# Counting TensorE's change of row count in an emission planner, and moving the adds of one norm's sums of squares

## The chip, the core and the metric

The kernel runs on one core of one Trainium2 chip. Five engines work side by side, each on its own queue in strict order: TensorE (matmuls and transposes, called PE in the profile, PEld for its weight loads), VectorE (DVE), ScalarE (ACT), GpSimd (POOL) and SyncE (SP), which issues the DMAs. The metric is the time of one execution on the device in microseconds. The time of a kernel is the median of several runs.

## The reference

Two layers over 512 tokens of width 1024, one after the other. Each layer takes a token norm, one input projection, a token mixer together with a cross-attention into 256 memory tokens, an output projection with a residual, and then a dense feed-forward with a norm of its own. The mixer of the first layer is chunked retention, that of the second differential attention with six heads of two 64-wide halves.

```python
def rms_norm(x, w):
    x32 = x.astype(jnp.float32)
    y = x32 * lax.rsqrt(jnp.mean(x32 * x32, axis=-1, keepdims=True) + EPS)
    return (y * w.astype(jnp.float32)).astype(x.dtype)
...
    for layer in range(DEPTH):
        h = rms_norm(x, attn_norm_w[layer])
        u = h @ w_in[layer]
...
        sc = jnp.einsum('bihcd,bjhcd->bhcij', qblk, k).astype(jnp.float32) * scale
        p = jax.nn.softmax(sc, axis=-1)
        a = p[:, :, 0] - lam * p[:, :, 1]
...
        x = x + jnp.concatenate([o_main, o_mem], axis=-1) @ w_out[layer]
        h = rms_norm(x, ffn_norm_w[layer])
        gu = h @ w_gate_up[layer]
        x = x + (jax.nn.silu(gu[..., :FFN_DIM]) * gu[..., FFN_DIM:]) @ w_down[layer]
```

All inputs are float32. The token norm sums squares over the 1024 features of each token.

## The kernel before

Activations lie transposed: eight tiles `xT[k]` of 128 features by 512 tokens. Every float32 factor is split into a rounded high part and a remainder (`split_h` on ScalarE, `split_l` mostly on VectorE), and a product is three matmuls: high by high, high by low, low by high (`mm3`). Weights come in chunks of up to 128x1024 through three raw pages (`wr`), are split into pages `wh` and `wl` (three each), and then used. The chunk after next can be loaded only when an earlier one has been split.

The order of the instructions on every engine is made by a planner when the program is written. `Weave` keeps an estimated clock for each engine. The main stream issues TensorE's projections; after each matmul of `mm3`, `W.pump()` runs every side stream (a Python generator: a split, a norm, an attention unit) whose due time lies no more than 0.1 us ahead of TensorE's estimated clock. The due times come from the estimated ends of earlier instructions plus a hand-over (`DELAY`). `Engine.go` (the estimate of TensorE stands at L269 to L271) gives each instruction its estimated duration: for a matmul with 64 rows (contracted partitions) 0.11 + 0.00012 n us, n its columns. Nothing of the estimate runs on the chip, where semaphores alone hold instructions back; but the estimate decides which instruction stands behind which.

Matmuls on 64 rows stand only in the second layer's differential attention: `unit` (L1132) computes the scores of one of six heads and one of four blocks of 128 queries, with both halves of a head in one call of `mm3_pair`: six matmuls, alternating between the upper and the lower 64 partitions. There are 24 such calls. Behind each follow a minimum on VectorE, two exponentials on ScalarE, a combination on VectorE, and for every second block transposes and the products with the values on TensorE. A `lane` starts the next unit only when VectorE's and ScalarE's estimated clocks are at most 4 us ahead of TensorE's (`W.backlog()`).

The first token norm is that of `norms[0]`, the only `NormX` with `later` set (4.0 us). For each tile `xT[k]`, `NormX.tile` (L613) splits the scaled tile into two `xw` pages, yields for `later`, draws one of three `tab` pages, squares the tile on ScalarE, and adds the square to the running sum, the first square's page, on GpSimd (L630). The planner's `take(tab=1)` keeps at most two further squares under way. After the eighth square `token_norm` multiplies the sum by ones on TensorE (eight small float32 passes) to sum over the features. The matmuls of the input projection meanwhile read the unnormed `xw`; the norm is applied behind them. The first block of the projection, `v1`, uses four chunks of 24 matmuls each.

`token_halves` (L1343) prepares operands for the feed-forward products of both layers: for each of four pairs of tiles, five intermediate results `z[0]` to `z[4]`, each half a `wk` page wide. It counts three pages, and draws six at L1357, since the page is drawn inside the inner loop.

Of the kernel before, what the change touches and what calls it, by code (L numbers as in the profile page):

```python
# [15 lines left out]
ALU = mybir.AluOpType  # L16
AX = mybir.AxisListType

P = 128
D = 1024  # L20
T = 512
# [128 lines left out]
def free_size(ap):  # L150
    n = 1
    for d in ap.shape[1:]:
        n *= d
    return n


class Weave:
# [7 lines left out]
    def __init__(self):  # L165
        self.n, self.q = 0, []
        self.clock = {"pe": 0.0, "dve": 0.0, "act": 0.0, "pool": 0.0, "dma": 0.0}
        self.written = {}
        self.slots, self.slot, self.seen = {}, {}, {}
        self.port = {"dve": [], "pool": []}  # L170
        self.last = self.cur = self.now = 0.0

    @property
# [80 lines left out]
class Engine:  # L254
# [5 lines left out]
    def __getattr__(self, op):  # L260
        call = getattr(self.engine, op)

        def go(out, *args, **kw):
            named = [v for k, v in kw.items() if isinstance(v, bass.AP) and k != "accum_out"]
            ins = [v for v in args if isinstance(v, bass.AP)] + named
            outs = [out] + [v for k, v in kw.items() if k == "accum_out"]
            n = free_size(ins[0] if op == "tensor_reduce" else out)
            if self.name == "pe":
                us = max(0.108, n / 2400 * (1 if op == "transpose" or kw["rhs"].dtype == F32R else 4) + 0.0134)  # L269
                if ins[0].shape[0] == 64:  # L270
                    us = 0.11 + 0.00012 * n  # L271
            elif self.name == "act":
                us = 0.09 + 0.00084 * n + 0.19 * ("accum_out" in kw) + 0.05 * isinstance(kw.get("scale"), bass.AP)
            elif self.name == "pool":
                us = 0.3 + 0.165 * n if kw.get("op") == ALU.pow else 0.17 + 0.0021 * n
            elif self.name == "dma":
                us = n * P * 4 / 360e3
            else:
                us = 0.07 + 0.00104 * n + 0.06 * any(free_size(v) == 1 and n > 1 for v in ins[1:])
            if self.name == "dma":  # L280
                self.weave.clock["dma"] = max(self.weave.clock["dma"], self.weave.t, self.weave.now)
            wide = [v for v in ins if free_size(v) > 1 or n == 1]
            here = [not v.tensor.name.startswith("ps_") for v in wide]
            double = sum(here) > 1 or op == "tensor_scalar" and all(here)
            port = self.name == "pool" or self.name == "dve" and double
            self.weave.run(self.name, us, outs, ins, port)
            return call(out, *args, **kw)  # L287

        return go
# [3 lines left out]
def body(ctx: ExitStack, tc: tile.TileContext, x_d, mem_d, w_d, par_d, dec_d, ali_d, out_d):  # L293
# [5 lines left out]
    V, A, G = Engine(W, "dve", nc.vector), Engine(W, "act", nc.scalar), Engine(W, "pool", nc.gpsimd)  # L299
# [8 lines left out]
    def page(tag, shape, bufs, dt=F32):  # L308
        z = sb.tile(shape, dt, tag=tag, name=nm(tag), bufs=bufs)
        W.page(tag, bufs, region(z[:, 0:1])[0])  # L310
        return z
# [12 lines left out]
    def take(**tags):  # L324
        n = tags.get("ps", 0)
        while True:
            if any(free[tag] < n_ for tag, n_ in tags.items()):
                yield 0.3
                continue
            due = max(heapq.nsmallest(n, banks), default=0.0) + 0.2  # L330
            if not n or due <= max(W.now, W.t) + EARLY:
                break
            W.cur = due
            yield
        for tag, n in tags.items():
            free[tag] -= n

    def give(tag, n):
        free[tag] += n
        if tag == "ps":  # L340
            for _ in range(n):
                heapq.heappush(banks, W.last)

    def wk(shape, dt=F32):
        return page("wk", shape, CAP["wk"], dt)
# [7 lines left out]
    def tab(shape):  # L353
        return page("tab", shape, 3)
# [35 lines left out]
    def col(c):  # L390
        return par[:, c:c + 1]
# [48 lines left out]
    def split(*parts):  # L440


        for dH, _, *src in parts:
            split_h(dH, *src)
        yield
        for p in parts:
            split_l(*p)
# [90 lines left out]
    def xw_page():  # L538
        return page("xw", [P, T], 2 * KT, F32R)
# [4 lines left out]
    def token_norm(srcs, ntok, out, bc=False, sq_sum=None, after=lambda: None):  # L544


        n = ntok // P
        if sq_sum is None:
            yield from take(tab=2)
            sq_sum = tab([P, T])  # L550
            A.activation(sq_sum, srcs[0], AF.Square)
            for src in srcs[1:]:
                sq = tab([P, T])
                A.activation(sq, src, AF.Square)
                yield
                G.tensor_tensor(sq_sum, sq_sum, sq, op=ALU.add)
            G.tensor_tensor(sq_sum[:, :ntok], sq_sum[:, :ntok], sq_sum[:, ntok:], op=ALU.add)
            give("tab", 1)
            after()
        W.cur = W.ready(sq_sum)  # L560
        yield
        yield from take(ps=1)
        pr = bank()
        for t in range(n):
            TE.matmul(pr[:, t:t + 1], lhsT=sq_sum[:, t * P:(t + 1) * P], rhs=ones[:, 0:1], start=True, stop=True)
        give("tab", 1)
        yield
        m, e, r = [page("r", [P, TT], 10)[:, :n] for _ in range(3)]
        V.tensor_scalar(m, pr[:, :n], 1.0 / D, EPS, op0=ALU.mult, op1=ALU.add)
        V.tensor_scalar(e, m, EPS, None, op0=ALU.mult)  # L570
        give("ps", 1)
        yield
        power(r, m, n)
        out.em, out.r = e, r
        if bc:
            yield from free_norm(out, out)
# [26 lines left out]
    class NormX:  # L603
# [9 lines left out]
        def tile(self, k):  # L613
            W.cur = W.ready(xT[k])
            yield
            h_, l_ = xw_page(), xw_page()
            yield from split((h_, l_, xT[k], col(self.c + k)))
            self.xw[k] = h_, l_
            while k > 0 and self.sums == 0:
                yield 0.3  # L620
            if self.later:
                yield self.later
            yield from take(tab=1)
            sq = tab([P, T])
            A.activation(sq, xT[k], AF.Square)
            if k == 0:
                self.sq_sum = sq
            else:
                yield
                G.tensor_tensor(self.sq_sum, self.sq_sum, sq, op=ALU.add)  # L630
                give("tab", 1)
            self.sums += 1
            if self.sums == KT:
                W.add(token_norm(None, T, self.nrm, self.bc, self.sq_sum), 0.0)
# [708 lines left out]
    def token_halves(layer, norm, tb):  # L1343


        room = []
        for tag, n, bufs in (("v", 3, 8), ("qc", KH, 2)):
            for z in [page(tag, [P, n, HT], bufs, F32R) for _ in range(bufs)]:
                room += [z[:, i, :] for i in range(n)]
        a, b = slice(0, HT), slice(HT, T)  # L1350
        def sums(j):
            while KH + j not in norm.xw:
                yield 0.5
            x1, x2 = xT[j], xT[KH + j]
            w1, w2 = col(norm.c + j), col(norm.c + KH + j)
            yield from take(wk=3)
            z = [wk([P, T])[:, s] for _ in range(3) for s in (a, b)]  # L1357
            A.activation(z[1], x1[:, b], AF.Copy, scale=w1)
            V.tensor_tensor(z[0], x1[:, a], x1[:, b], op=ALU.subtract)
            yield  # L1360

            V.scalar_tensor_tensor(z[2], x2[:, b], w2, z[1], op0=ALU.mult, op1=ALU.subtract)
            V.scalar_tensor_tensor(z[3], x1[:, a], w1, z[2], op0=ALU.mult, op1=ALU.add)
            V.scalar_tensor_tensor(z[4], x2[:, a], w2, z[3], op0=ALU.mult, op1=ALU.subtract)
            parts = [(room.pop(), room.pop(), *src) for src in ((z[0], w1), (z[2],), (z[3], -1.0), (z[4], -1.0))]
            yield
            for part in parts:
                yield from split(part)
            give("wk", 3)
            tb[j] = [part[:2] for part in parts]  # L1370

        for j in range(KH):
            W.add(sums(j), 0.0)
            yield 3.0
# [358 lines left out]
```

## Time and profile before

| | us |
|---|---|
| median of 3 runs | 1141.38 |
| lowest and highest run | 1139.38 and 1141.46 |
| profiled execution, its own time | 1143.51 |
| profiled execution, span from first to last instruction | 1141.7 |

| engine | busy us | share of the span |
|---|---|---|
| PE | 1130.7 | 99% |
| DVE | 892.6 | 78% |
| ACT | 626.8 | 55% |
| POOL | 157.8 | 14% |

The span lies 1.8 us under the profiled execution's own time, and that time 2.1 us above the median. A row of the timeline gives the start, the duration, the engine, the operation with what it writes and reads, how many like it stand together, and in brackets the idle time before it and what ended that. Durations of matmuls are modelled and overlap: the distance from one start to the next tells more. A row of the stretches gives each engine's busy time with its instructions, the clock granted to TensorE (1.00 is 2.4 GHz, 0.50 is 1.2 GHz) and the DMA's share.

### The profile page before, as it was taken

To read this page: it belongs to the slowest core of one execution; us is meant where nothing else is said; L and a number is where in the kernel's file an instruction comes from. 1 tells how busy PE (TensorE), PEld (TensorE's weight loads), DVE (VectorE), ACT (ScalarE), POOL (GpSimd) and SP (SyncE) were. 2 spreads that over 40 slices of the span, in tenths; PEclk is the share of its full clock that TensorE was granted. 3 is DMA by queue.
4 is the path that set the end of the run, shared out by engine and by line. 5 is a ranking of instruction groups with operands and counts; after the bars stand their busy time and mean duration, and the time that the engine had idled before them with its cause. 6 is when DMAs were issued, how large, how long until landed. Compare 5 with 4: busy or idle time off the path is not lost.

```text
span 1141.7 us, 18447 instructions
## 1 busy us (share of the span) xinstructions
PE 1130.7 (99%) x6917; PEld 999.2 (88%) x6917; DVE 892.6 (78%) x1717; ACT 626.8 (55%) x1291; POOL 157.8 (14%) x105
## 2 busy tenths in 40 slices
PE   9999999999999999999999999999999999999998
PEld 7788888889999999998888877888899999999987
DVE  5669895799997878887657577967989987788862
ACT  6557773545564445555466575745556554455540
POOL 4120010400000000000362653343000000000000
PEclk9999999999999999999999999999999999999999
DMA  6341222332342333334231311122332333223332
GB/s 212 126 143 61 74 74 75 111 93 92 118 136 84 103 110 102 97 112 159 68 116 58 111 61 51 57 74 93 94 108 89 125 105 123 86 93 102 96 111 76
DMA packets 46600, 113.54 MB, mean 99 GB/s; under 512 B 5296, under 2 KB 17968, under 8 KB 46512
## 3 DMA queue, kind: packets, MB, share of 16 engines
q1 hardware_dynamic: 46368, 112.35, 30.5%
q8 instruction: 54, 0.88, 0.3%
q14 instruction: 34, 0.28, 0.1%
q10 hardware_dynamic: 144, 0.03, 0.0%
HBM read 110.26 MB, written 2.10 MB: 98 GB/s over the span
## 4 chain that ended last, share of the span: by engine, by line
PE 91%; DVE 3%; ACT 3%; POOL 1%; issue 1%; DMA 1%; SPq 0%; DVEq 0%; ACTq 0%
PE ps L287 91%; DVE wk L287 1%; POOL tab L287 1%; ACT wk L287 1%; DVE sm L287 1%; DMA wr<-w_t 1%; ACT wh L287 0%; DVE qk L287 0%; ACT qk L287 0%; ACT mkY L287 0%; DVE mkL L287 0%; SPq L287 0%; ACT L287 0%; ACT qc L287 0%; ACT xw L287 0%
## 5 line engine op out<-in xcount | busy, mean ns | idle before, releaser
L287 PE MATMUL ps<-xw,wh 128*128 128x256 f32 (+1 forms) x1032 | 211.6, 326 | 0.0
L287 ACT ACTIVATE wk<-ps 128x256 f32<-128x256 f32 (+3 forms) x214 | 90.8, 427 | 168.2 <-PE ps L287 167.2
L287 PE MATMUL ps<-xw,wl 128*128 128x256 f32 (+1 forms) x948 | 179.0, 306 | 0.0
L287 PEld LDWEIGHTS ps<-xw,wh 128*128 128x128 f32 x1032 | 154.4, 190 | 15.5
L287 PE MATMUL ps<-wh,xw 128*128 128x512 f32 (+1 forms) x512 | 151.1, 375 | 1.0 <-DVE qk L287 1.0
L287 PEld LDWEIGHTS ps<-xw,wl 128*128 128x128 f32 x948 | 131.2, 190 | 7.4
L287 PE MATMUL ps<-qk,wl 128*128 128x512 f32 (+1 forms) x528 | 135.6, 386 | 0.0
L287 ACT ACTIVATE wh<-wr 128x512 fp32r<-128x512 f32 (+1 forms) x144 | 118.6, 827 | 27.2 <-PE ps L287 20.9
L287 DVE TENSOR_TENSOR wl<-wk,wl 128x512 fp32r<-128x512 f32 (+3 forms) x150 | 94.4, 630 | 29.0 <-ACT wl L287 28.2
L287 PEld LDWEIGHTS ps<-qk,wl 128*128 128x128 f32 x528 | 96.1, 188 | 18.3
L287 ACT ACTIVATE wl<-wk 128x512 fp32r<-128x512 f32 (+3 forms) x150 | 85.6, 571 | 40.1 <-DVE wk L287 25.7
L287 PEld LDWEIGHTS ps<-wh,xw 128*128 128x128 f32 x512 | 92.8, 191 | 16.5 <-DVE qk L287 1.5
L287 POOL TENSOR_TENSOR tab<-tab,tab 128x512 f32<-128x512 f32 x31 | 47.2, 1524 | 431.9 <-DVE v L287 306.7
L287 PE MATMUL ps<-v,wh 128*128 128x256 f32 x792 | 106.1, 279 | 0.0
L287 PE MATMUL ps<-qk,wh 128*128 128x512 f32 (+1 forms) x393 | 104.4, 387 | 0.5 <-DVE qk L287 0.5
L287 DVE TENSOR_TENSOR wh<-wk,wh 128x512 fp32r<-128x512 f32 (+3 forms) x130 | 79.2, 609 | 26.7 <-ACT wh L287 26.7
L287 PEld LDWEIGHTS ps<-v,wh 128*128 128x128 f32 x792 | 98.3, 189 | 0.0
L287 PE MATMUL ps<-wl,xw 128*128 128x512 f32 (+1 forms) x256 | 96.0, 375 | 0.9 <-DVE wl L287 0.9
L287 ACT ACTIVATE wh<-wk 128x512 fp32r<-128x512 f32 (+3 forms) x130 | 72.6, 559 | 42.5 <-DVE wk L287 34.6
L287 DVE TENSOR_TENSOR xT<-ps,xT 128x512 f32<-128x512 f32 (+1 forms) x81 | 55.1, 680 | 50.9 <-PE ps L287 50.6
L287 PEld LDWEIGHTS ps<-qk,wh 128*128 128x128 f32 x393 | 71.9, 188 | 15.6 <-DVE qk L287 1.1
L287 PE MATMUL ps<-v,wl 128*128 128x256 f32 x576 | 77.4, 279 | 0.0
(169 smaller groups left out, 1969.7 us busy)
## 6 DMA issues: line engine op xcount, KB each, us to landing
wr<-w_t SPq DMA_DIRECT2D x148, 512.0 KB, 3.5
wk<-w_t SPq DMA_DIRECT2D x48, 192.0 KB, 3.8
wk<-w_t SPq DMA_DIRECT2D x32, 256.0 KB, 3.9
wk<-w_t SPq DMA_DIRECT2D x32, 128.0 KB, 3.4
wr<-w_t SPq DMA_DIRECT2D x8, 256.0 KB, 5.2
xT<-x_t SPq DMA_DIRECT2D x8, 256.0 KB, 5.5
zo<-mem_t SPq DMA_DIRECT2D x8, 256.0 KB, 6.0
out_t<-xT SPq DMA_DIRECT2D x7, 256.0 KB, 2.0
```

Source lines behind the costliest of these rows:

```text
L287: return call(out, *args, **kw)
```

## The change

Three edits. The planner's estimate of a TensorE instruction grows by 0.19 us whenever its row count differs from that of the instruction ahead of it. The running sum of squares of the first token norm is added by VectorE in place of GpSimd; the other three such norms keep GpSimd. `token_halves` draws three pages and uses both halves of each.

```diff
@@ Weave.__init__
+        self.rows = 128
@@ Engine.go
                 if ins[0].shape[0] == 64:
                     us = 0.11 + 0.00012 * n
+
+                us += 0.19 * (ins[0].shape[0] != self.weave.rows)
+                self.weave.rows = ins[0].shape[0]
@@ NormX.tile
-                G.tensor_tensor(self.sq_sum, self.sq_sum, sq, op=ALU.add)
+                (V if self.later else G).tensor_tensor(self.sq_sum, self.sq_sum, sq, op=ALU.add)
                 give("tab", 1)
@@ token_halves
-            z = [wk([P, T])[:, s] for _ in range(3) for s in (a, b)]
+            z = [w[:, s] for w in [wk([P, T]) for _ in range(3)] for s in (a, b)]
```

## Rows read from the trace of the kernel before

**Rows 1.** The page's first part: busy time and share of the span.

```profile
PE 1130.7 (99%) x6917; PEld 999.2 (88%) x6917; DVE 892.6 (78%) x1717; ACT 626.8 (55%) x1291; POOL 157.8 (14%) x105
```

**Rows 2.** Stretches: length; busy PE, PEld, DVE, ACT, POOL; clock; DMA share; GB/s.

```profile
23.00:27.00 4.00, 2.80 (x13) 1.90 (x13) 3.56 (x3) 2.30 (x3) 2.52 (x2) 0.88 0.36 92
27.00:33.00 6.00, 6.00 (x15) 4.74 (x16) 2.98 (x8) 1.54 (x6) 2.04 (x2) 0.51 0.73 248
80.00:135.00 55.00, 53.45 (x280) 44.49 (x279) 50.78 (x101) 40.12 (x89) 4.11 (x4) 1.00 0.26 87
200.00:230.00 30.00, 30.00 (x138) 24.93 (x137) 22.50 (x33) 16.68 (x31) 12.50 (x8) 1.00 0.38 114
255.00:520.00 265.00, 265.00 (x1917) 250.31 (x1916) 228.07 (x420) 140.30 (x291) 0.00 (x0) 1.00 0.33 105
640.00:765.00 125.00, 123.24 (x769) 98.84 (x769) 99.10 (x293) 82.36 (x223) 57.13 (x32) 1.00 0.23 72
```

**Rows 3.** Timeline of TensorE, 20 to 34 us.

```profile
22.53 0.62 PE L287 MATMUL ps<-wh,xw 128*128 128x512 f32 x2
...
23.21 0.74 PE L287 MATMUL ps<-wh,xw 128*128 128x512 f32 x2
24.52 0.50 PE L287 MATMUL ps<-wl,xw 128*128 128x512 f32 x1 [0.57 <-DVE wl L287]
25.66 1.52 PE L287 MATMUL ps<-ones,tab 128*128 128x1 f32 x8 [0.63 <-POOL tab L287]
27.03 1.20 PE L287 MATMUL ps<-wh,xw 128*128 128x512 f32 x2
...
33.04 0.39 PE L287 MATMUL ps<-wl,xw 128*128 128x512 f32 x1
```

**Rows 4.** Timeline of ScalarE, 8 to 45 us.

```profile
21.42 0.61 ACT L287 ACTIVATE wh<-wr 128x512 fp32r<-128x512 f32 x1
22.25 0.63 ACT L287 ACTIVATE tab<-xT 128x512 f32<-128x512 f32 x1 [0.22 <-POOL tab L287]
22.79 2.51 ACT L287 ACTIVATE wh<-wr 128x512 fp32r<-128x512 f32 x3
```

**Rows 5.** Timeline of VectorE, 8 to 45 us.

```profile
15.96 0.99 DVE L287 SCALAR_TENSOR_TENSOR xw<-xT,par,xw 128x512 fp32r<-128x512 f32 x1 [0.72 <-ACT xw L287]
22.07 0.70 DVE L287 TENSOR_TENSOR wl<-wr,wh 128x512 fp32r<-128x512 f32 x1 [5.11 <-ACT wh L287]
23.43 4.38 DVE L287 TENSOR_TENSOR wl<-wr,wh 128x512 fp32r<-128x512 f32 x3 [0.67 <-ACT wh L287]
```

**Rows 6.** Timeline of GpSimd, 8 to 45 us.

```profile
14.88 10.72 POOL L287 TENSOR_TENSOR tab<-tab,tab 128x512 f32<-128x512 f32 x7 [13.57 <-ACT tab L287]
```

**Rows 7.** VectorE's groups by shape, 22 to 28 us, then 190 to 230.

```profile
L287 DVE TENSOR_TENSOR wl<-wr,wh 128x1024 fp32r<-128x1024 f32 x2 | 3.4, 1750 | 0.0
...
L287 DVE TENSOR_TENSOR wl<-wr,wh 128x1024 fp32r<-128x1024 f32 x7 | 8.5, 1219 | 0.4 <-ACT wh L287 0.4
```

**Rows 8.** Tile tab, VectorE: count, shortest, median and longest ns.

```profile
L287 DVE TENSOR_TENSOR wk<-wk,tab x38: 691/692/694, 265.5 to 1099.7; 128x512 f32<-128x512 f32 x38
```

**Rows 9.** The chain of work that ended last: start, length, what.

```profile
14.80 0.07 issue
```

**Rows 10.** Timeline of TensorE, 223 to 227 us.

```profile
224.60 0.95 PE L287 MATMUL ps<-ones,tab 128*128 128x1 f32 x8
225.41 0.49 PE L287 MATMUL ps<-xw,wl 128*128 128x512 f32 x1
```

**Rows 11.** Timeline of TensorE, 655 to 662 us.

```profile
656.91 0.39 PE L287 MATMUL ps<-wl,xw 128*128 128x512 f32 x1
657.23 0.79 PE L287 MATMUL ps<-qk,qk 64*128 64x384 f32 x6
657.95 0.73 PE L287 MATMUL ps<-wh,xw 128*128 128x512 f32 x2
658.52 0.27 PE L287 MATMUL ps<-ident,wk 128*128 128x128 f32 x1
```

## The prediction

> **What bounds the kernel now.** I read the page first: TensorE is busy 99% of the span, so only three things can move the time: TensorE's own work, stretches where it waits, and its clock [rows 1]. The change removes no matmul. I then cut the span into stretches and looked for TensorE idle time and a granted clock below 1.00 [rows 2]. The long feed-forward stretches (255 to 520 us stands for both layers) hold no idle time at all; VectorE is busy for 228 of those 265 us, but beside TensorE. Idle time stands in three places. From 80 to 135 us there are 1.55 us of it, spread over several waits. From 640 to 765 us, the second layer's differential attention, there are 1.76 us. And between 23 and 33 us something larger happens: 1.2 us of idle time in four microseconds, and then six microseconds at a granted clock of 0.51, that is almost all of it on the lower level, 1.2 GHz. It is the only stretch of the table far below 1.00.
>
> The timelines of that stretch tell why. TensorE runs three 512-column matmuls in 0.68 us, 0.227 us each, until 23.2 us; then it waits for a weight remainder from VectorE, then at 25.66 us for the sums of squares from GpSimd, and from 27.03 us on each matmul takes twice as long, up to 32.5 us or so [rows 3]. On ScalarE the squares of the token norm (tile tab) and the splits of the weights (tile wh) share one queue. Only three tab pages exist, one of them the running sum, so a square waits until GpSimd has added an earlier one; the split of the fourth weight chunk stands behind such squares and starts only at 21.42 us, its second half at 22.79 us [rows 4]. VectorE sits idle for 5.11 us before that, waiting for this split, and then needs 4.38 us for three remainders [rows 5]. GpSimd's seven adds take 10.72 us from 14.88 us on, 1.53 us each [rows 6]. While GpSimd adds, VectorE's own work on two SBUF operands is slower as well: a 128x1024 remainder took 1.75 us in this stretch and 1.22 us in another [rows 7]. So one chain, seven slow adds, sets the late weights, the late norm and, behind both, the fallen clock.
>
> **The adds move from GpSimd to VectorE** (the condition on `later` holds for the first token norm alone). Gone: seven adds of 1.53 us. New: seven VectorE adds of two SBUF tiles of 128x512; the nearest rows are 38 instructions of this shape at 0.69 us [rows 8]. From the first add at 14.88 us: seven adds at 0.69 us are 4.8 us, seven hand-overs of 0.07 us (the gap that the chain of waits shows between the end of a square and GpSimd's add [rows 9]; I take it for VectorE too) 0.5 us, and one input split of 0.99 us that VectorE has to do in between [rows 5]: the last sum is there at about 21.2 us, against 25.6 us. VectorE has the room, in its 5.11 us of waiting. Behind the adds, which now wait for ScalarE's squares, stand on VectorE's queue that input split and the remainders of the fourth chunk. TensorE needs that chunk at about 22.5 us, its second half at 23.2 us; the squares ahead of the split then wait for adds of 0.69 us, so the split should come near 20 us and the remainder near 21.5 us, a margin of about one microsecond. GpSimd has nothing else until the power of the norm, and no DMA is moved past another.
>
> What TensorE gets back: from 23.21 to 27.03 us stand three 512-column matmuls and eight small ones of the norm. At the upper clock the same eight took 0.81 us in the next norm [rows 10], so the stretch needs 0.68 + 0.81 = 1.49 us of 3.82 us: 2.3 us back. From 27.03 to 33.04 us stand 14 matmuls (five rows of two and four rows of one on the timeline, of which the first and the end are shown); 14 x 0.227 = 3.2 us of 6.0 us: 2.8 us back if the clock stays up. Together **5.2 us**. The bounds: nothing, if TensorE waits there all the same; 5.2 us plus the 1.55 us of idle time behind it, if the earlier norm also eases those waits. I take 5.2 us because the wait that starts the chain has one cause and the cause is cut by more than half. What is late next: the weights of the next chunks, whose loads start when these splits end; they move forward with them. Whether other small waits of the first layer change I cannot derive, since emission places shift: between -1.5 and +1.5 us, from the idle time of 80 to 135 us [rows 2]; I take zero.
>
> **The estimate of TensorE** (`us += 0.19` at each change of the row count) makes no instruction cheaper. It shifts the planner's clock, and so the places at which side work is put among TensorE's matmuls. Matmuls on 64 rows stand only in `unit` of the second layer: six for each of 24 calls, with a change before and behind, so 48 x 0.19 = 9.1 us are added to the planner's clock. Is the new estimate better? For the six of 384 columns the code before says 6 x (0.11 + 0.00012 x 384) = 0.94 us. In the trace the block takes 0.72 us from its first start to the next matmul's; the matmul ahead of it 0.32 us in place of 0.227, and the two behind it 0.57 us in place of 0.45: 0.72 + 0.09 + 0.12 = 0.93 us [rows 11]. The old estimate is right for this block as it stands, and the new one, 1.32 us, is 0.38 us too long. A planner that thinks TensorE later than it is puts dependent work earlier among the matmuls; the cover between a unit's scores and its transposes loses 0.38 us for each other unit in between, which is one, mostly. Against that stands that all the other small waits of this stretch are in no estimate either, so a slower clock may fit the whole better than it fits the block. Bounds: a gain of 1.76 us at most, the idle time that is there [rows 2]; a loss of 9.1 us at most. I take +1.0 us, near the lower end, because this stretch now waits for 1.4% of its time and there are 12 pairs of units, a few of which would lose 0.38 us.
>
> The Trainium skill has a rule that speaks against the new estimate: matmuls on different row groups of the array run at the same time (TensorE: Matmul & The Clock Gate, Part 3: Packing small matmuls). By it six matmuls of 384 columns on two halves would cost as much as three, an estimate of 0.51 us, and the new figure would be 0.81 us too long, 19 us over 24 units, which would make the loss larger. The trace agrees in part: 0.72 us, less than six times 0.17 us but more than three times [rows 11]. The sum does not use this.
>
> **Pages of `token_halves`.** Three pages are drawn where six were, with the same accounting. Nothing is computed otherwise. At worst two halves on one page order a VectorE step behind a ScalarE copy of about half a microsecond, four times a layer; this lies in the feed-forward's start, where TensorE is busy for all of the 30 us from 200 us on [rows 2]. Cost nil; without that cover up to 8 x 0.5 = 4 us. A gain is excluded by TensorE's being busy throughout.
>
> **The sum.** Profiled execution 1143.5 us: -5.2 + 1.0 = 1139.3 us. It lies 2.1 us above the median of the three runs, so the prediction for the median is 1141.4 - 4.2 = **1137.2 us**.
>
> **Rivals.** (A) The attention pays it back. If the new clock leaves most dependent steps without cover, TensorE waits in 640 to 765 us by up to 9.1 us more; 9.1 - 5.2 = +3.9, so 1145.3 us. It decides from 7.5 us of new waits on (5.2 + 2.3). For it: the block's rows; against it: no more than 1.76 of 125 us are idle now, so most dependent steps have cover, if of unknown size. (B) The wait shrinks but the clock falls all the same, because a shorter wait at the norm or at the fourth chunk remains: only 2.3 us back, 1139.1 us. For it: a margin of one microsecond, with VectorE's queue strict in order. (C) The change does not do what it says: the split of the fourth chunk is late for its place in ScalarE's queue, not for GpSimd, and TensorE waits as before: 1141.4 us. Against it: the squares ahead of it wait visibly for GpSimd. (D) The new places fit better and the attention's idle time goes as well: -5.2 - 1.8, so 1134.4 us. For it: the other waits that no estimate holds.
>
> **How the numbers follow.** Forecast 62%, with its own range of 1134.5 to 1140; A 9%, B 12%, C 7%, D 10%. The range leaves out A and tails on both sides: 1134 to 1142 us. A measurement here tells about 0.2% (2.3 us) from no change. Faster than 1139.1 us: most of the forecast (54%), half of B, all of D, some 0.69. Within: the rest of the forecast, half of B, most of C and a part of A, 0.23. Slower: most of A and a little of C, 0.08.
>
> **What would show it.** Right: no seven adds on GpSimd at 15 to 25 us; the last square's add near 21 us; the split of the fourth chunk on ScalarE near 20 us; a granted clock of 1.00 from 23 to 33 us and the chunk behind it started some 5 us earlier; the same matmul counts. Wrong in the first step: TensorE waits for tab or wl near 23 us again. Wrong in the second: more than 2.8 us of idle time in the attention's 125 us.

## The result and the profile after

The changed kernel is slower: 1146.18 us (1145.90 to 1147.21, 6 runs) against 1139.57 us (1139.11 to 1141.46, 6 runs), a ratio of 1.0057 with a 95% interval of 1.0047 to 1.0068. The forecast was 1137.2 us and faster. The profiled execution of the changed kernel took 1145.9 us, 0.3 us under its median; that of the kernel before took 1143.51 us, which with three more runs at hand stands 3.9 us above its median. The median of the kernel before thus stands 1.8 us lower than with the three runs that the forecast went by. That matters below.

Stretches of the changed kernel (columns as in [rows 2]), at its start and in the attention, in the place of the rows of before:

```profile
23.00:27.00 4.00, 4.00 (x20) 3.30 (x19) 0.61 (x3) 1.24 (x3) 0.00 (x0) 1.00 0.63 215
27.00:33.00 6.00, 6.00 (x30) 4.93 (x29) 5.16 (x13) 4.89 (x14) 3.34 (x3) 1.00 0.57 183
250.00:515.00 265.00, 265.00 (x1918) 250.32 (x1917) 228.20 (x420) 140.27 (x291) 0.00 (x0) 1.00 0.33 105
635.00:768.00 133.00, 126.63 (x773) 100.32 (x772) 103.09 (x295) 83.72 (x224) 56.67 (x33) 1.00 0.22 68
```

From 23 to 33 us the start looks as forecast: full clock, no idle time where [rows 2] had 1.2 us of it and a clock of 0.51. The feed-forward is what it was. The attention has 6.4 us of idle time in 133 us, against 1.76 us in 125 [rows 2].

Timeline of VectorE at the start of the changed kernel, against [rows 5] and [rows 6]:

```profile
13.90 1.48 DVE L291 TENSOR_TENSOR tab<-tab,tab 128x512 f32<-128x512 f32 x2
15.30 0.74 DVE L291 SCALAR_TENSOR_TENSOR xw<-xT,par,xw 128x512 fp32r<-128x512 f32 x1
15.96 3.08 DVE L291 TENSOR_TENSOR tab<-tab,tab 128x512 f32<-128x512 f32 x4
18.96 0.69 DVE L291 TENSOR_TENSOR wl<-wr,wh 128x512 fp32r<-128x512 f32 x1
19.71 0.69 DVE L291 TENSOR_TENSOR tab<-tab,tab 128x512 f32<-128x512 f32 x1
```

The seven adds take 0.68 to 0.70 us each, the input split between them takes 0.74 us (0.99 us in [rows 5]), and the last sum is there at 20.4 us. ScalarE splits the fourth chunk from 18.02 us on, where [rows 4] had 21.42 and 22.79.

To see where the time went I took a mark that both kernels have: the eight small matmuls of the norms. Timeline of TensorE, changed kernel, the first layer's feed-forward norm and the second layer's:

```profile
220.07 0.95 PE L291 MATMUL ps<-ones,tab 128*128 128x1 f32 x8
...
803.70 0.95 PE L291 MATMUL ps<-ones,tab 128*128 128x1 f32 x8
```

From the first of these to the last, 583.6 us pass. In the profiled execution of before they start at 224.60 [rows 10] and 801.35 us:

```profile
801.35 0.95 PE L287 MATMUL ps<-ones,tab 128*128 128x1 f32 x8
```

That is 576.75 us. So the profile says: 4.5 us won before the first mark, 6.9 us lost between them, where the attention lies. Yet -4.5 + 6.9 = 2.4 us is not the 6.6 us of the medians. Both terms needed a test.

### The profile page after: what moved, and what is told of

Same layout as the page of the kernel before. It is cut to its first block, busy times and chain, and to the rows that moved or that the text cites. A ratio compares the mean times of both kernels' runs of the same rounds, so it can differ in the third digit from the quotient of the medians.

```text
span 1144.1 us, 18456 instructions
## 1 busy us (share of the span) xinstructions
PE 1129.5 (99%) x6917; PEld 997.2 (87%) x6917; DVE 898.9 (79%) x1724; ACT 626.8 (55%) x1291; POOL 147.3 (13%) x98
## 4 chain that ended last, share of the span: by engine, by line
PE 88%; DVE 5%; ACT 5%; issue 2%; DMA 0%; SPq 0%; ACTq 0%; DVEq 0%
PE ps L291 88%; DVE wk L291 3%; ACT wk L291 2%; DVE qk L291 1%; DVE sm L291 1%; ACT qk L291 1%; ACT wh L291 1%; DMA wr<-w_t 0%; ACT mkY L291 0%; DVE mkL L291 0%; ACT tab L291 0%; ACT qc L291 0%; ACT L291 0%; SPq L291 0%; ACT xw L291 0%
## 5 line engine op out<-in xcount | busy, mean ns | idle before, releaser
L291 ACT ACTIVATE wk<-ps 128x256 f32<-128x256 f32 (+4 forms) x214 | 90.3, 427 | 167.0 <-PE ps L291 166.1
L291 POOL TENSOR_TENSOR tab<-tab,tab 128x512 f32<-128x512 f32 x24 | 37.0, 1541 | 418.6 <-ACT tab L291 418.0
```

## Which edit

The diffs from here on show the lines that matter. Left out are lines that set up and advance `rows`, the row count of TensorE's last instruction, and `n64`, which counts the matmuls on 64 rows that have been written (144 in all, six for each of the 24 units).

Theory: the added 0.19 us costs the attention its 7 us, and the adds on VectorE win the head's. Rivals: the edits disturb the attention together, or the adds cost the time.

**The estimate alone.** Edits two and three undone:

```diff
-                (V if self.later else G).tensor_tensor(self.sq_sum, self.sq_sum, sq, op=ALU.add)
+                G.tensor_tensor(self.sq_sum, self.sq_sum, sq, op=ALU.add)
...
-            z = [w[:, s] for w in [wk([P, T]) for _ in range(3)] for s in (a, b)]
+            z = [wk([P, T])[:, s] for _ in range(3) for s in (a, b)]
```

> The planner's 0.19 us alone; adds on GpSimd and six pages as before. Theory (the estimate costs the time, the head's gain is separate): the attention loses what the two traces show, 6.9 us between the second and the fourth norm, and the head keeps its wait, so 1145 to 1148 us against some 1139.6. Rival 1 (the three edits disturb the attention together, as the emission of one shifts the next): this one alone gives less than half, under 1143 us. Rival 2 (the adds cost the time): no change, 1139.6 us.

Measured: 1146.52 us against 1139.44, ratio 1.0068 (1.0055 to 1.0080). That is all of the loss: the interval overlaps that of the changed kernel (1.0047 to 1.0068).

**The adds alone.** Kernel before with the line in `NormX.tile` as in the change:

```diff
-                G.tensor_tensor(self.sq_sum, self.sq_sum, sq, op=ALU.add)
+                (V if self.later else G).tensor_tensor(self.sq_sum, self.sq_sum, sq, op=ALU.add)
```

> The first norm's seven adds on VectorE alone. Theory: the wait of 2.3 us near 25 us goes, the attention stays as in the kernel before, so 2 us under the kernel before, up to 5 us where its clock fell behind the wait: 1135 to 1138 us. Rival 1 (the edits disturb the attention together): between 1138 and 1143 us. Rival 2 (the adds cost the time): 1143 us or more.

Measured: 1139.12 us, ratio 0.9997 (0.9989 to 1.0006). They neither cost nor win anything that can be told. The 5.2 us of the forecast are not there, and the expected 1135 to 1138 us were missed.

**The pages alone.**

```diff
-            z = [wk([P, T])[:, s] for _ in range(3) for s in (a, b)]
+            z = [w[:, s] for w in [wk([P, T]) for _ in range(3)] for s in (a, b)]
```

> Three pages drawn in place of six in the feed-forward's start alone. Theory: nothing, within 0.2% of the kernel before (1137.3 to 1141.9 us), since TensorE does not wait there. Rival (page rotation shifts the emission of the attention, which follows): up to 3 us either way, and idle time of TensorE in the attention other than 1.8 us.

Measured: 1139.37 us, ratio 1.0003 (0.9994 to 1.0013), with the attention's 1.73 us of idle time unchanged. Nothing, as forecast.

**Adds and pages, without the estimate.**

```diff
-                us += 0.19 * (ins[0].shape[0] != self.weave.rows)
-                self.weave.rows = ins[0].shape[0]
```

> The adds on VectorE and the three pages, without the 0.19 us. Theory: as with the adds alone, 1135 to 1138 us. Rival (edits disturb the attention together): it differs from the run with the adds alone by over 2 us.

Measured: 1139.65 us, ratio 1.0004 (0.9995 to 1.0012). The expected win is missing here too, and these two edits do not disturb each other.

## Where the head's 5 us went

**The kernel before, once more,** without an edit.

> The kernel before, unchanged, for a second profile of its first 40 us. Reading 1 (the wait near 25 us and the fallen clock were of that one execution, which was 4 us over the median): granted clock 1.00 from 27 to 33 us, under 1 us of idle time from 23 to 33 us, second norm near 71.5 us as in the runs that leave the head alone. Reading 2 (the head always loses it): clock near 0.5 again and the second norm near 76 us.

Measured: 1139.15 us. Reading 1 holds. Stretches of this execution at the same places as [rows 2]:

```profile
23.00:27.00 4.00, 3.54 (x20) 2.75 (x19) 3.97 (x6) 1.69 (x4) 1.63 (x2) 1.00 0.57 140
27.00:33.00 6.00, 6.00 (x29) 4.74 (x28) 4.47 (x12) 4.42 (x13) 3.53 (x4) 1.00 0.89 305
```

The same program, and no fallen clock: 1.00 where [rows 2] shows 0.51, and one wait of 0.46 us for the sums in place of the long one. The norm of the memory tokens (four small matmuls, the "second norm" of the expectation) starts at 71.65 us on TensorE, that of the changed kernel at 71.47, that of the profiled execution of before at 76.05. Timeline of TensorE in this execution, then in the profiled one of before:

```profile
24.39 1.05 PE L287 MATMUL ps<-ones,tab 128*128 128x1 f32 x8 [0.46 <-POOL tab L287]
71.65 0.59 PE L287 MATMUL ps<-ones,tab 128*128 128x1 f32 x4
```

```profile
76.05 0.59 PE L287 MATMUL ps<-ones,tab 128*128 128x1 f32 x4
```

In the changed kernel the wait for the sum is still there, earlier and shorter, 0.28 us in place of 0.46:

```profile
20.46 1.05 PE L291 MATMUL ps<-ones,tab 128*128 128x1 f32 x8 [0.28 <-DVE tab L291]
```

What differs between the two executions of before is the first 10 us. Timeline of ScalarE in this execution, then in the profiled one of before:

```profile
5.99 2.01 ACT L287 ACTIVATE xw<-xT,par 128x512 fp32r<-128x512 f32 x3
20.14 0.62 ACT L287 ACTIVATE wh<-wr 128x512 fp32r<-128x512 f32 x1
```

```profile
7.48 2.06 ACT L287 ACTIVATE xw<-xT,par 128x512 fp32r<-128x512 f32 x3 [1.18 <-DMA xT<-x_t]
```

In the execution that the prediction read, tiles of the input landed late and ScalarE waited 1.18 us for them; everything on ScalarE and GpSimd came some 1.3 us later, the fourth chunk's split at 21.42 in place of 20.14 us, while TensorE had begun at the same time. In that execution the wait of 0.46 us grew, and the clock fell behind it. The chain of [rows 4 to 6] is real, but in a usual execution it ends nearly in time, so that making it faster wins next to nothing.

Thirteen profiled executions leave this start as it was (this one, and those of the runs without the adds on VectorE). In all of them the clock is 1.00 in both stretches, and the norm of the memory tokens starts at 71.4 to 73.0 us. The latest is that of the run with 0.06 us below, where tiles landed late again. Its ScalarE, and its stretches:

```profile
7.54 2.06 ACT L291 ACTIVATE xw<-xT,par 128x512 fp32r<-128x512 f32 x3 [1.63 <-DMA xT<-x_t]
```

```profile
23.00:27.00 4.00, 2.82 (x14) 1.79 (x15) 3.50 (x3) 2.36 (x3) 2.57 (x2) 1.00 0.34 96
27.00:33.00 6.00, 6.00 (x30) 4.72 (x29) 4.51 (x12) 3.79 (x12) 3.05 (x3) 1.00 0.83 258
```

So late tiles are not confined to one execution. With the same 1.2 us of idle time the clock stayed up there, and the delay at the norm of the memory tokens is 1.3 us (72.98 us) in place of 4.4 us. Why tiles land late in some executions, and why the clock fell in one of the two, the runs do not tell.

## What the estimate does to the attention

The waits of TensorE in the attention, changed kernel, then the kernel before once more (who waited for whom: us in total, times, longest):

```profile
PE ps L291 <- DVE wk L291: 3.8, 6, 1.1
PE ps L291 <- DVE sm L291: 1.8, 2, 1.6
PE ps L291 <- DVE zo L291: 0.5, 1, 0.5
```

```profile
PE ps L287 <- DVE qk L287: 1.0, 1, 1.0
PE ps L287 <- ACT wk L287: 0.6, 3, 0.2
PE ps L287 <- DVE wk L287: 0.2, 1, 0.2
```

Waits for the softmax results (wk) and for the small sums and scales (sm) stand at the top. Most of the sm share is one wait of 1.59 us, for a small VectorE instruction that stood beside a GpSimd subtraction (last section). It is there in the run with the estimate alone too, 1.59 us again, and in neither profile of the kernel before: the new order put the two side by side. Between the two marks, 4.6 of the 6.9 us are idle time of TensorE (7.49 us, against 2.86 in the kernel before once more); the other 2.3 us are counted as busy, with the same number of matmuls within one, and their place stays open. The first pair of units shows how a wait for wk comes about. Timeline of TensorE, changed kernel:

```profile
650.29 0.62 PE L291 MATMUL ps<-qk,qk 64*128 64x256 f32 x6
650.84 0.50 PE L291 MATMUL ps<-wl,xw 128*128 128x512 f32 x1
651.18 0.64 PE L291 MATMUL ps<-wh,xw 128*128 128x512 f32 x2
651.66 0.40 PE L291 MATMUL ps<-wl,xw 128*128 128x512 f32 x1
651.99 0.79 PE L291 MATMUL ps<-qk,qk 64*128 64x384 f32 x6
652.71 0.50 PE L291 MATMUL ps<-wh,xw 128*128 128x512 f32 x1
653.04 0.27 PE L291 MATMUL ps<-ident,wk 128*128 128x128 f32 x1
654.39 0.44 PE L291 MATMUL ps<-ident,wk 128*128 128x128 f32 x2 [1.07 <-DVE wk L291]
```

And the kernel before once more, the same pair:

```profile
650.73 0.62 PE L287 MATMUL ps<-qk,qk 64*128 64x256 f32 x6
651.28 0.74 PE L287 MATMUL ps<-wh,xw 128*128 128x512 f32 x2
651.87 0.40 PE L287 MATMUL ps<-wl,xw 128*128 128x512 f32 x1
652.10 0.63 PE L287 MATMUL ps<-wh,xw 128*128 128x512 f32 x2
652.57 0.39 PE L287 MATMUL ps<-wl,xw 128*128 128x512 f32 x1
652.89 0.79 PE L287 MATMUL ps<-qk,qk 64*128 64x384 f32 x6
653.61 0.73 PE L287 MATMUL ps<-wh,xw 128*128 128x512 f32 x2
654.18 0.27 PE L287 MATMUL ps<-ident,wk 128*128 128x128 f32 x1
654.60 0.44 PE L287 MATMUL ps<-ident,wk 128*128 128x128 f32 x2 [0.16 <-DVE wk L287]
```

Between the scores and their transposes stand five projection matmuls in place of eight. From the scores to the second row of transposes some 4 us pass in both (650.29 to 654.39, and 650.73 to 654.60): the wait for wk ends both, so that is what ScalarE and VectorE need. With three matmuls fewer, 0.68 us, TensorE waits 1.07 us in place of 0.16. Over the whole stretch I summed these other matmuls from the written order of TensorE's instructions (columns over 2.4 GHz plus 13 ns each, which gives the 0.227 us of a 512-column matmul; between each of the 12 last score blocks of a pair and its transposes): 65 us in the kernel before, 43 us in the changed one.

The next runs ask what rule this follows. For all of them, the idle time of TensorE in three stretches of the attention, read from the rows of the stretches as length less busy time:

| kernel | median us | ratio (95%) | idle 640 to 700 | 700 to 735 | 735 to 770 |
|---|---|---|---|---|---|
| before, once more | 1139.15 | | 1.55 | 0.19 | 0.00 |
| changed kernel | 1146.18 | 1.0057 (1.0047 to 1.0068) | 3.03 | 2.06 | 1.28 |
| estimate alone, 0.19 | 1146.52 | 1.0068 (1.0055 to 1.0080) | 3.03 | 1.73 | 1.45 |
| 0.06 | 1142.89 | 1.0027 (1.0018 to 1.0037) | 0.67 | 0.92 | 1.60 |
| -0.10 | 1144.19 | 1.0042 (1.0030 to 1.0055) | 0.00 | 0.07 | 3.19 |
| spread over TensorE | 1146.20 | 1.0059 (1.0046 to 1.0073) | 2.22 | 2.32 | 0.58 |
| 0.19, transposes later | 1147.41 | 1.0067 (1.0054 to 1.0080) | 2.61 | 2.45 | 1.20 |
| 0.19, others 1.10 | 1141.63 | 1.0016 (1.0007 to 1.0025) | 1.61 | 0.86 | 0.89 |
| -0.10 up to unit 16 | 1143.73 | 1.0033 (1.0021 to 1.0046) | 0.00 | 0.08 | 3.67 |
| -0.10 up to unit 12 | 1140.11 | 1.0008 (0.9999 to 1.0016) | 0.00 | 1.78 | 0.58 |
| all engines 1.13 | 1145.09 | 1.0052 (1.0039 to 1.0064) | 0.00 | 0.37 | 4.87 |
| others 1.10 alone | 1150.22 | 1.0091 (1.0078 to 1.0105) | 0.00 | 3.29 | 6.95 |
| -0.10 up to unit 8 | 1138.15 | 0.9987 (0.9978 to 0.9996) | 0.19 | 0.30 | 0.00 |

**A third of it.** The estimate alone, with 0.06 us:

```diff
-                us += 0.19 * (ins[0].shape[0] != self.weave.rows)
+                us += 0.06 * (ins[0].shape[0] != self.weave.rows)
```

> Kernel before with 0.06 us in place of 0.19 us at each change of the row count. In the written order of TensorE's instructions, the other matmuls between a unit's scores and its transposes sum, over the 12 groups of transposes, to 65 us in the kernel before, to 43 us with 0.19 us and to 60 us here (columns over 2.4 GHz plus 13 ns each). Theory (lost cover becomes waiting): the loss follows the cover, so 7.1 x 5/22 = 1.6 us over the kernel before, 1140 to 1142.5 us. Rival (any shift of the planner's clock breaks up a tuned order): over 1143 us.

Measured: 1142.89 us, just over the upper end of the theory and just under the rival's bound. A loss that is smaller than with 0.19 us. Not all of it belongs to the estimate: the profiled execution (1142.92 us, 3.8 us over that of the kernel before once more) lost 1.3 us at the start, where tiles landed late, and 2.1 us between the two marks (578.86 us against 576.72). The theory's price for the lost cover was 1.6 us. How many of the other eight runs had the late tiles is not known.

**The other sign.** The estimate alone, with -0.10 us:

```diff
-                us += 0.19 * (ins[0].shape[0] != self.weave.rows)
+                us += -0.10 * (ins[0].shape[0] != self.weave.rows)
```

> Kernel before with -0.10 us at each change, so that the blocks of 64 rows count as too short. The cover of the transposes is 63 us in the written order, against 65 us before. Theory (lost cover): no loss worth telling, 1138.5 to 1141 us. Rival (any shift breaks a tuned order): over 1143 us. Third reading (the old estimate was already too long): faster by up to 1.8 us.

Measured: 1144.19 us, in the rival's range. By the time alone the theory falls. The place of the waits says more: 0.07 us of idle time in the first 95 us, then this (stretches of that run):

```profile
735.00:740.00 5.00, 2.51 (x15) 1.67 (x14) 4.93 (x17) 3.52 (x13) 2.94 (x2) 0.85 0.68 241
740.00:745.00 5.00, 5.00 (x24) 4.03 (x24) 4.75 (x18) 2.65 (x9) 1.01 (x1) 0.50 0.09 38
```

The dependent steps have cover for 95 us; at the end VectorE is busy for 4.93 of 5 us and TensorE waits for its results: half of the stretch idle, then five microseconds at a clock of 0.50. I read this as two ways to lose: steps placed too early, which wait one by one, and steps placed too late, which pile up at the end.

**The same time, spread.** The kernel before, with TensorE's 128-row instructions between the first and the last 64-row matmul 1.13 times as long by the estimate:

```diff
+                    self.weave.n64 += 1
+                elif 0 < self.weave.n64 < 144:
+                    us *= 1.13
```

> Kernel before, the matmuls on 64 rows estimated as before, but every TensorE instruction on 128 rows between the first and the last of them at 1.13 times its estimate: about the same 9.1 us in all, spread over other instructions. Cover of the transposes 39 us. Theory (a planner's clock of TensorE that is too slow, wherever the time is put): a loss at least as large as with the 0.19 us, 1146 to 1149 us. Rival (it matters that the time is put at the scores themselves): within 2 us of the kernel before.

Measured: 1146.20 us, within the theory's interval. The loss does not need the time to be put at the change of rows.

**Only the transposes later.** The estimate alone, and in `unit`:

```diff
                 yield 0.3
+            yield 1.0
 
             yield from take(ps=u + 1)
```

> The 0.19 us alone, and in each unit of the attention the transposes fall due 1.0 us later by the planner's clock. Their cover in the written order is 61 us again (65 before, 43 with the 0.19 us alone). Theory (the transposes come too early): most of the 7.1 us is back, 1139.5 to 1142.5 us. Rival (units start too early, so VectorE is overrun whatever the place of the transposes): 1144.5 us or more.

Measured: 1147.41 us, in the rival's range. The cover of the transposes was back (61 us in the written order) and nothing was won: TensorE now waits for other steps, 2.0 us for the keys and queries (qk) and 1.8 us for the normed heads (zo), 1.6 us for wk. My theory that the transposes carry the loss falls with this, and so does lost cover as a measure of the loss; other dependent steps wait in their place.

**All other engines slower too.** The estimate alone, and for VectorE, ScalarE and GpSimd in the stretch (`n64` counted as above):

```diff
+            if self.name in ("act", "dve", "pool") and 0 < self.weave.n64 < 144:
+                us *= 1.10
```

> The 0.19 us alone, and from the first to the last matmul on 64 rows the planner's estimates of VectorE, ScalarE and GpSimd are 1.10 times as long too, so that the engines' clocks keep their proportion. Cover of the transposes in the written order 50 us (65 before, 43 with the 0.19 us alone). Theory (a clock of TensorE that is too slow against the other engines puts every dependent step too early): between a third and two thirds of the 7.1 us is back, 1141.5 to 1144.5 us. Rival (any shift breaks a tuned order): 1144.5 us or more.

Measured: 1141.63 us: 4.9 us of the 7.1 are back by lengthening three more estimates. That speaks for the relation of the clocks to each other and against the rival that any shift does harm; the run with all engines at 1.13, below, will speak the other way.

**The other sign, for a part of the units.** The kernel before, with -0.10 us up to the 16th unit:

```diff
+                if self.weave.n64 < 97:
+                    us -= 0.10 * (ins[0].shape[0] != self.weave.rows)
+                self.weave.rows = ins[0].shape[0]
```

> Kernel before with -0.10 us at each change of the row count, but only up to the 16th of the 24 units. With -0.10 us throughout, TensorE waited 0.07 us in the first 95 us of the attention and then 3.2 us in the last 35, where its clock fell too. Theory (a fast clock of TensorE gives cover early and leaves work without cover at the end): the early part stays free of waits, the end is eased, 1137.5 to 1141 us. Rival (any shift breaks a tuned order): 1143 us or more.

Measured: 1143.73 us, missed, and in the rival's range: nearly free of waits to 735 us (0.08 us), and 3.67 us in the last part.

And up to the 12th unit:

```diff
-                if self.weave.n64 < 97:
+                if self.weave.n64 < 73:
```

> As the run up to the 16th unit, but up to the 12th of the 24. Theory: the units behind are placed by the old estimate, so the end has its old cover: 1137 to 1140 us, the best of the three with a shorter estimate. Rival (any shift breaks a tuned order): 1143 us or more.

Measured: 1140.11 us, just over the expected interval: the end is down to 0.58 us, but 1.78 us stand in the middle.

**All engines 1.13.** The spread of above, and the other three engines with it:

```diff
+            if self.name in ("act", "dve", "pool") and 0 < self.weave.n64 < 144:
+                us *= 1.13
```

> All engines slow alike: between the first and the last matmul on 64 rows, TensorE's instructions on 128 rows and everything on VectorE, ScalarE and GpSimd at 1.13 times their estimates. The same as the run with the time spread over TensorE, but for the other engines. Theory (the proportion of the clocks counts): over half of that run's loss of 6.8 us is back, 1139 to 1142.5 us. Rival (any shift breaks a tuned order): 1143 us or more.

Measured: 1145.09 us, missed, and in the rival's range. The time was not won back, but the waits changed sides: none in the first 60 us, where the spread alone had 2.22, and 4.87 us at the end. TensorE's 64-row blocks and the hand-overs were not stretched, so this planner may hold TensorE for too fast; that is a reading after the fact, and no run tests it.

**The others slower, TensorE as before.**

```diff
+            if self.name in ("act", "dve", "pool") and 0 < self.weave.n64 < 144:
+                us *= 1.10
```

> TensorE's estimates as before; VectorE, ScalarE and GpSimd 1.10 times as long in the stretch. This is the other side: TensorE's clock counts as too fast. Theory: hardly any wait of TensorE in the first 60 us of the attention (under 0.3 us against 1.6 us before), work left without cover in the last 35, as with -0.10 us: 1141 to 1146 us. Rival (any shift breaks the order anywhere): waits spread over the whole stretch.

Measured: 1150.22 us, more than expected. The waits are where they were expected in the first 60 us (none) and in the last 35 (6.95 us, at a clock of 0.85); 3.29 us in the middle were not expected:

```profile
640.00:700.00 60.00, 60.00 (x342) 47.05 (x341) 41.03 (x128) 36.43 (x101) 29.09 (x16) 1.00 0.25 80
700.00:735.00 35.00, 31.71 (x243) 26.93 (x241) 32.52 (x97) 24.77 (x72) 16.98 (x9) 1.00 0.18 60
735.00:770.00 35.00, 28.05 (x164) 22.72 (x165) 23.61 (x64) 17.26 (x44) 8.43 (x7) 0.85 0.16 47
```

**A gain by the same rule.** The first 8 of the 24 units:

```diff
-                if self.weave.n64 < 97:
+                if self.weave.n64 < 49:
```

> Kernel before with -0.10 us at each change of the row count up to the 8th of 24 units, to beat both kernels: with -0.10 us up to the 12th the first 60 us were free of waits and the next 35 lost 1.8 us. Theory: the waits of the first 60 us stay away (-1.6 us) and the middle has its old places, 1137 to 1139.5 us. Rival (any shift breaks a tuned order): over 1141 us.

Measured: 1138.15 us, ratio 0.9987 (0.9978 to 0.9996), faster than both kernels. Stretches of that run:

```profile
640.00:700.00 60.00, 59.81 (x341) 46.59 (x341) 43.44 (x134) 36.37 (x103) 29.15 (x16) 1.00 0.26 80
700.00:735.00 35.00, 34.70 (x267) 29.59 (x264) 33.60 (x107) 26.90 (x79) 13.31 (x8) 1.00 0.15 46
735.00:770.00 35.00, 35.00 (x196) 28.53 (x195) 23.30 (x55) 18.78 (x39) 11.65 (x7) 1.00 0.20 60
```

Idle time is 0.49 us in 130, against 1.74 us in the kernel before, and the time fell by 1.5 us. It is the last of four choices of the same kind, so this one number is weak evidence for the rule behind it.

**What is shown and what is open.** Shown: the estimate alone makes the loss, by another order of the same instructions. Three runs with TensorE's planned clock slowed against the others (0.19, spread, 0.19 with later transposes) wait 2.2 to 3.0 us in the first 60 us, where the kernel before waits 1.55; five with it sped up (the four of -0.10 and 1.10 alone) wait at most 0.19 us there, and all but one of these pay in the middle or at the end. The run with 0.06 us does not fit: its clock is slowed too, and it waits 0.67 us in the first 60 us and 1.60 at the end. Not settled: the rule as a whole, and the size. That nearly every shift lost time fits also with an order that was good by selection; three runs ended in that rival's range (-0.10, -0.10 up to unit 16, all engines 1.13), and three well under it (0.19 with the others at 1.10, -0.10 up to unit 12 and up to unit 8).

## Why the prediction was wrong

- **The sum.** The forecast lay 9.0 us too low: some 4.9 us for a gain of the adds that is not there and 6.1 us for the attention, less 1.8 us by which the median of three runs (1141.38 us) stood above that of six (1139.57 us).
- **The bound.** TensorE's idle time and clock were the right things to read, and the attention was named. That holds. The list of three idle places was not complete (0.87 us stand between 580 and 590 us of the same trace), which changes nothing in the sum.
- **The adds, cost.** Right: 0.68 to 0.70 us each, 6.5 us from the first to the last (6.3 forecast). That the last sum came at 20.4 us (21.2 forecast) and the split of the fourth chunk at 18.0 us (20 forecast) owes about a microsecond to tiles that landed in time. The full clock from 23 to 33 us came as forecast, but not by the adds: the kernel before, run once more, has it too.
- **The adds, gain: -5.2 us. Wrong.** The run with the adds alone measures -0.3 us with an interval that holds zero. The step that failed is taking the stretch of one execution [rows 2, 3] for that of the runs. The wait for the sums that the adds were to remove is 0.46 us in the kernel before once more, and 0.28 us of it is left with the adds on VectorE. The prediction noted that this execution was 2.1 us above the median and then took the offset off the total, as if it lay everywhere. It lay in this very stretch: the clock of 0.51, 2.8 us of the 5.2 us, was an event of that execution alone among fourteen with this start, and more than half of the remaining 2.3 us comes of its late tiles, which cost 1.3 us in the run with 0.06 us. Rival B had the clock as a condition, but assumed that it falls always.
- **The estimate: +1.0 us. Wrong in size, right in sign.** It costs 7.1 us. Its mechanism, dependent work that stands too early, is seen in the first pair of units. The arithmetic on the block held: the old estimate fits it [rows 11], the new one is too long. The prediction's own sign of being wrong here, more than 2.8 us of idle time, came: 6.4 us. The step that failed is the price: 0.38 us for each other unit in between and "a few" of 12 pairs. The planner moves whole matmuls; the lost cover was 22 us over 12 pairs, not 0.38 us for a few, and other steps than the transposes waited as well, 1.59 us of it for a VectorE instruction beside one of GpSimd. The bound of 9.1 us held, and the value was taken from the wrong end of it: no run with a slower clock of TensorE alone was faster, though the prediction hoped that such a clock "may fit the whole better". How the 7.1 us divide among the moved steps stays open, since giving the transposes their cover back won nothing.
- **Rival A**, 1145.3 us, is what happened (1146.18), at a chance of 9%. It was priced on top of the head's gain, from a median that was too high, and so came out near partly by luck: 9.1 - 5.2 = 3.9 us, where 7.1 - 0.3 was measured.
- **The pages.** Nil, as forecast (ratio 1.0003).

## What to carry to other kernels

A profiled execution that is slower than the median has its excess somewhere; look for it in the stretch from which you mean to win, and do not price a gain from waits or a fallen clock that a second profile does not show. In a planner that interleaves side work by estimated clocks, an order is not made better by one correct-looking term of an estimate. In most of these runs it was the clock of the filled engine against those of the engines that feed it that told where the waits came (from the start on: dependent steps too early; piled up at the end: too late). Take such changes one at a time and measure them: neither the microseconds of the term nor the matmuls that left the gap gave the size of the loss.

## What the chip showed besides

A VectorE instruction on four elements of each partition took 2.02 us in the changed kernel; the same one takes 0.16 us at the median. It ended within 0.02 us of a GpSimd subtraction of 128x1024 that ran beside it, and TensorE's longest wait in the attention of that run, 1.59 us, follows directly. Timelines of VectorE, GpSimd and TensorE:

```profile
687.26 2.02 DVE L291 SCALAR_TENSOR_TENSOR sm<-sm,sm 128x4 f32<-128x4 f32 x1
```

```profile
686.89 2.37 POOL L291 TENSOR_TENSOR wl<-wr,wh 128x1024 fp32r<-128x1024 f32 x1 [2.76 <-ACT wh L291]
```

```profile
689.63 0.73 PE L291 MATMUL ps<-qk,qk 64*128 64x256 f32 x6 [1.59 <-DVE sm L291]
```

The Trainium skill (GPSIMD Engine Reference, 8. Key points) says that GpSimd shares its SBUF interfaces with VectorE, with contention when the VectorE instruction has two SBUF inputs. The trace agrees: two more VectorE instructions on 128x4 ran beside such a subtraction in this trace, for 1.72 us from 680.84 us on and 1.43 us from 725.54 us on, and both ended within 0.05 us of it; without one beside them such instructions take 0.15 or 0.16 us. In each case the small instruction ran until the large one was done.

TensorE's clock fell once behind an idle share that looks small: 1.2 us idle in four microseconds at the start of one execution [rows 2]. The same idle time at the same place left it at 1.00 in the run with 0.06 us, and so did a single wait of 1.07 us in the attention of the changed kernel. What decides between them these runs do not show.
